# A two-layer trunk on one core: the low part of every third weight chunk made by ScalarE and an accumulating DMA

## The chip, the cores and the metric

One Trainium2 chip, one of its cores. The metric is the device time of one execution in microseconds (us), lower is better. The kernel before takes 1078.44 us (median of 2 runs, 1078.35 to 1078.53).

## What is computed

A trunk of two layers on 256 tokens of 1024 numbers in float32. Each layer is a SwiGLU, a mixer (differential attention in layer 0, retention in layer 1) and a second SwiGLU, each behind an RMS norm and added to the residual:

```python
h = x + 0.5 * _swiglu(_rms(x, ffn1_norm[i]), ffn1_w_in[i], ffn1_w_out[i])
xn = _rms(h, mix_norm[i])
m = _diff_attention(xn, ...) if kind == 0 else _retention(xn, ...)
h = h + m
x = h + 0.5 * _swiglu(_rms(h, ffn2_norm[i]), ffn2_w_in[i], ffn2_w_out[i])

def _swiglu(xn, w_in, w_out):            # w_in 1024 x 5632, w_out 2816 x 1024
    a, b = jnp.split(xn @ w_in, 2, axis=-1)
    return (jax.nn.silu(a) * b) @ w_out
```

Nearly all of the work is `x @ w` with a weight that is read once.

## The kernel before

**Products.** A float32 product is made of three products in float32r, a rounded format that TensorE takes at a higher rate. Both factors are split exactly: `hi` is the rounded value, `lo` is what is left of it. The sum is x_hi w_hi + x_lo w_hi + x_hi w_lo (`mm_tokens`, `mm_cols`; every matmul is issued at L263). In the SwiGLU's first product (`mm_cols`) the weights are stationary, and x_hi and x_lo stand side by side as 512 moving columns, so a block of 128 x 128 weights takes one matmul of 512 columns with `hi` and one of 256 with `lo`.

**Weights.** `Weights` (L96 to L173) cuts all weights into 180 chunks of 1 MB, 128 partitions by 2048 numbers, in the order of their use: chunk 0 and 1 are split in four pieces, the others in two pieces of 128 x 1024. Chunks 0 to 32 belong to the first SwiGLU (names f0: 22 chunks of `w_in`, which come in pairs, then 11 of `w_out`), 33 to 48 to the attention, 49 to 81 and 82 to 114 to the SwiGLUs f1 and f2, 115 to 146 to the retention, 147 to 179 to f3. There are three sets of buffers, four of each: `raw` (what the DMA loads from HBM), `hi` and `lo`. Chunk i goes through these steps:
- `load` (L120): SyncE's queue issues one DMA of 1 MB into `raw`; it needs the raw buffer of chunk i-4, that is, both pieces of that chunk have been split. `keep_order` holds SyncE to the order of issue, so a load that waits holds up those behind it.
- `round` (L136): ScalarE casts a piece of `raw` into `hi` (L150). The buffer was that of chunk i-4, so TensorE has to be done with that one.
- `remain` (L153): VectorE subtracts, lo = raw - hi (L157). After the last piece the raw buffer is given back and the next load is issued.
- `take`: TensorE's stream uses the chunk.

When each step is issued is decided while the program is written: `Flow` keeps an estimate of the time of TensorE's stream, and `paced` splits a further piece every 800 ns of it as far as there are buffers; `take` forces what is still missing. A scheduler then sets the order on each engine; an engine takes its instructions in that order, and one that waits holds up those behind it.

**SwiGLU.** For a pair of chunks (gate columns `wa`, value columns `wb`, 256 columns each) TensorE makes four passes of 16 matmuls: `pa`, `pb`, `pa`, `pb`, each into a bank of PSUM of its own (8 banks). Behind each pass ScalarE copies half of the bank (`rest`, L316) and VectorE adds the halves (L317); ScalarE applies SiLU (L469), VectorE multiplies (L477), and the result is split into `hT` (L311 on ScalarE, L312 on VectorE). Then `out_proj` multiplies with `w_out`, adds to the residual `h` (L411), and squares it (L333) for the next norm.

**Norm.** In `norm_transpose` VectorE adds the sums of squares (`v`, L351), GpSimd takes the power -0.5 (`r`, L343), VectorE scales (`xs`, L357), TensorE transposes (`pt`, L293), and the result is split into `xn`, which every product of the next part needs. A token tile's norm is done behind the last product of that tile. The norms of the attention's heads and of the retention use the same line L343. GpSimd does nothing else in the kernel before but set constants.

**Opening.** From 0 to about 36 us the order is written out by hand: chunks 0 and 1 in four pieces, the two norms, then chunks 2 and 3, whose products (`pa`, `pb`) follow the first `ps_f` products of chunks 0 and 1.

Of the kernel before, what the change touches and what calls it, by code (L numbers as in the profile page):

```python
# [15 lines left out]
ALU = mybir.AluOpType  # L16
# [4 lines left out]
T = 256  # L21
# [10 lines left out]
ROOT_D = 32.0  # L32
TAIL = 2

# Offsets in the table of constants: distances, decays.
C_DIST = 0
C_DEC = 384
C_END = C_DEC + RT_H * 384


def constants():
    """Causal distances (masked ones far away) for the query tiles side by side, and the
    retention's decays by head, keys on the partitions: key tile 0 with all queries, then
    key tile 1 with query tile 1."""
    c = np.zeros((P, C_END), np.float32)
    p = np.arange(P)[:, None]
    k = np.arange(T)[None, :]
    for off, n, q0 in ((0, P, 0), (P, T, P)):
        d = (q0 + p) - k[:, :n]
        c[:, C_DIST + off : C_DIST + off + n] = np.where(d >= 0, d, FAR)  # L50
    for h in range(RT_H):
        log_g = math.log(1.0 - 2.0 ** (-5.0 - h))
        d = k - p
        dec = np.where(d >= 0, np.exp(np.maximum(d, 0) * log_g), 0.0) / 16.0
        at = C_DEC + h * 384
        c[:, at : at + T] = dec
        c[:, at + T : at + 384] = dec[:, :P]
    return c


class Flow:
    """Order of issue: the main stream of products says how long each takes, and tasks (generators
    that yield the time their next step has to wait) are taken up in between when they are due."""

    def __init__(self):
        self.now, self.tasks, self.n = 0.0, [], 0
# [27 lines left out]


class Weights:  # L96
    """Chunks of the weights in the order of their use: loaded ahead, and split exactly into two
    float32r parts ahead, piece by piece, as far as there are buffers."""

    RAW, PARTS, PACE = 4, 4, 800  # L100

# [26 lines left out]
            self.raws.append(raw)  # L128

    def split(self):  # L130
        """Split a further piece if a buffer for it is there."""
        if self.round():
            self.remain()
            self.next = self.flow.now + self.PACE

    def round(self):  # L136
        if not self.todo:
            i = len(self.parts)
            if i >= min(len(self.specs), self.freed + self.PARTS):
                return False  # L140
            self.load()
            _, shape, pieces = self.specs[i]
            hi = self.pool.tile([P] + shape, F32R, tag="hi", name=f"hi{i}", bufs=self.PARTS)
            lo = self.pool.tile([P] + shape, F32R, tag="lo", name=f"lo{i}", bufs=self.PARTS)
            n = shape[0] // pieces
            self.todo = [(i, slice(k, k + n)) for k in range(0, shape[0], n)]
            self.parts.append((hi, lo))
        i, ks = self.todo.pop(0)
        self.rounded.append((i, ks, not self.todo))
        self.nc.scalar.copy(self.parts[i][0][:, ks, :], self.raws[i][:, ks, :])  # L150
        return True

    def remain(self):  # L153
        i, ks, last = self.rounded.pop(0)
        hi, lo = self.parts[i]
        raw = self.raws[i]
        self.nc.vector.tensor_tensor(lo[:, ks, :], raw[:, ks, :], hi[:, ks, :], ALU.subtract)  # L157
        if last:
            self.raws[i] = None
            self.load()  # L160
# [17 lines left out]


def keep_order(tc, start, *engines):  # L180
    """These engines (or all) take what has been issued since start in that order."""
    before = {}
    dep = mybir.DependencyInfo(mybir.DependencyClass.NoSync, mybir.DependencyReason.DATA)
    for ins in issued(tc)[start:]:
        if engines and ins.engine not in engines:
            continue
        if ins.engine in before:
            tc.add_manual_dep(ins, before[ins.engine], dep, reason="order")
        before[ins.engine] = ins.name
# [3 lines left out]
def trunk_kernel(ctx: ExitStack, tc: tile.TileContext, io, out: bass.AP):  # L193
# [15 lines left out]
    def blk(name, dtype, shape):  # L209
        return blkp.tile([P] + shape, dtype, tag="blk", name=name)  # L210

# [1 line left out]
    h = [act.tile([P, D], F32, tag=f"h{t}", name=f"h{t}") for t in range(NT)]  # L213

    def load_x(t):
# [11 lines left out]
    ones = const.tile([1, P], F32, name="ones")  # L227
    nc.vector.memset(ones, 1.0)

# [1 line left out]
    def plan_ffn(w_in, w_out):  # L231
        for j in range(FF // 256):
            pieces = 2 if wts.specs else 4
# [10 lines left out]
    w = io["da_w_in"][0]  # L244
# [6 lines left out]
    w = io["rt_w_in"][0]  # L251
# [6 lines left out]
        wts.rows(io["rt_w_out"][0], 2 * c)  # L258
    plan_ffn(io["ffn2_w_in"][1], io["ffn2_w_out"][1])

# [1 line left out]
    def mm(ps, lhsT, rhs, start, stop):  # L262
        nc.tensor.matmul(ps, lhsT=lhsT, rhs=rhs, start=start, stop=stop)  # L263
        flow.tick(7 + rhs.free_size() / 2.4 if lhsT.dtype == F32R else 7 + rhs.free_size() / 0.6)
# [1 line left out]
    xn = [None]  # L266

    def mm_tokens(ps, t, part, k0, nk, first, last):
        """ps[tokens, cols] += x[tokens, k0..] @ w, weights moving."""
        hi, lo = part  # L270
        for k in range(nk):
            xh = xn[0][:, k0 + k, t * P : (t + 1) * P]
            xl = xn[0][:, k0 + k, T + t * P : T + (t + 1) * P]
            mm(ps, xh, hi[:, k, :], first and k == 0, False)
            mm(ps, xl, hi[:, k, :], False, False)
            mm(ps, xh, lo[:, k, :], False, last and k == nk - 1)

    def mm_cols(ps, part, c):
        """ps[cols, 0:T] + ps[cols, T:2T] = (x @ w).T for 128 columns, weights stationary."""
        hi, lo = part  # L280
        cs = slice(c * P, (c + 1) * P)
        for k in range(KD):
            both = [
                (ps, hi[:, k, cs], xn[0][:, k, :], k == 0, k == KD - 1),
                (ps[:, :T], lo[:, k, cs], xn[0][:, k, :T], False, False),
            ]
            for args in reversed(both) if k == KD - 1 else both:
                mm(*args)
# [6 lines left out]
        return pt  # L295

    def proj_tokens(each, before=(None, None)):
        """x @ 512 columns by token tile; each(t, ps) takes the bank over."""
        ws = [wts.take() for _ in range(2)]
        for t in range(NT):  # L300
            if before[t] is not None:
                flow.join(before[t])
            ps = bank(f"pj{flow.n}_{t}")
            for i, part in enumerate(ws):
                mm_tokens(ps, t, part, 4 * i, 4, i == 0, i == 1)
                if t == NT - 1:
                    wts.free()
            each(t, ps)
# [7 lines left out]
        nc.scalar.copy(rest, ps[:, T:])  # L316
        nc.vector.tensor_tensor(out_ap, ps[:, :T], rest, ALU.add)  # L317

# [1 line left out]
    def load_gain(src, scale=1.0, n=D, tag="gain"):  # L320
        g = work.tile([P, n], F32, tag=tag, name=f"g{flow.n}_{src.tensor.name}", bufs=1)
        nc.sync.dma_start(g, src.partition_broadcast(P))
# [47 lines left out]
            flow.urgent -= 1  # L370

    def out_proj(nk, src, coef, name, gain, last=False):
        """h += coef * src @ w; begins the norm of h for the next part."""
        nch = nk // 2
        pieces = [[(0, 512), (512, 512)] for _ in range(NT)]
        if last:
# [15 lines left out]
        for c in range(nch - TAIL):  # L392
            part = wts.take()
# [5 lines left out]
        tasks = []  # L399
# [20 lines left out]
                tasks.append(flow.spawn(norm_transpose(t, xn[0], halves, name)))  # L420
        return tasks

# [1 line left out]
    def ffn(name, before, next_gain, last=False):  # L424
        hT = []

# [58 lines left out]
            last,  # L485
        )

# [1 line left out]
    def attention(before, next_gain):  # L489
        dist = const.tile([P, 384], F32, name="dist")  # L490
        nc.sync.dma_start(dist, io["consts"][:, C_DIST : C_DIST + 384])
# [19 lines left out]
        nc.vector.tensor_scalar(nlam, le[:, 1:2], le[:, 0:1], LAM_INIT, ALU.subtract, ALU.subtract)  # L511

        def grouped_norm(ps, ng, dim, name, w0, w1):
            """ps / rms over groups of dim columns, short of sqrt(dim)."""
            sq = work.tile([P, 512], F32, tag="xs", name=f"sq_{name}")
            nc.scalar.activation(sq, ps, AF.Square)
            ss = small.tile([P, ng], F32, tag=f"ss{ng}", name=f"ss_{name}")
            nc.vector.tensor_reduce(ss, sq.rearrange("p (g d) -> p g d", d=dim), AX.X, ALU.add)
            nc.vector.tensor_scalar_add(ss, ss, dim * EPS)
            r = inv_rms(ss, ng, name)  # L520
            yield w0
            qn = work.tile([P, 512], F32, tag="xs", name=f"qn_{name}")
            nc.vector.tensor_tensor(
                qn.rearrange("p (g d) -> p g d", d=dim),
                ps.rearrange("p (g d) -> p g d", d=dim),
                r.unsqueeze(2).broadcast_to([P, ng, dim]),
                ALU.mult,
            )
            yield w1
            return transposes(f"ptn_{name}", qn, 4).rearrange("p (j c) -> p j c", c=P)  # L530
# [16 lines left out]
        sides = (slice(0, P), slice(P, 384))  # L547

        def head(g, hh, qT, kT, need, wait, res):
            """One head's probabilities, transposed."""  # L550
            yield wait
            flow.join(*need)
            slope = 2.0 ** (-8.0 * (g * 4 + hh + 1) / DA_H)
# [2 lines left out]
            for m in range(2):  # L556
                name = f"{g}{hh}{m}"
                ms = slice(m * DH, (m + 1) * DH)
                ps = bank(f"s_{name}")
# [25 lines left out]
            a = work.tile([P, 384], F32, tag="att", name=f"att_{g}{hh}")  # L585
# [13 lines left out]
        aTs, oT = {}, {}  # L599

        def values(g, v, need, outs):
            """The heads' outputs, normed, transposed and split."""
            po = [bank(f"po_{g}{t}") for t in range(NT)]
            for hh in range(4):
                flow.join(need[hh])
# [28 lines left out]
        heads = {}  # L634
# [18 lines left out]

        return out_proj(KD, src, 1.0, "dao", next_gain)

# [1 line left out]
    def retention(before, next_gain):  # L657
        mT, done = [], []

        def mix(hd, v, qk, sg, sub, dec, pair):  # L660
            """One head's outputs, normed, gated, transposed and split."""
            yield 4000
            sT = bank(f"sT_{hd}")
            for cs, ks, qs in (
# [3 lines left out]
                for dk in range(2):  # L668
# [4 lines left out]
                        start=dk == 0,  # L673
# [53 lines left out]
        for hd in range(RT_H):  # L727
# [9 lines left out]
            for i in range(2):  # L737
                part = wts.take()
# [95 lines left out]
```

## Time and profile before

| | us |
|---|---|
| median of the runs | 1078.44 |
| the profiled execution: span from its first to its last instruction | 1076.2 |
| TensorE matmuls busy | 1065.4 (99%) |
| VectorE busy | 687.2 (64%) |
| ScalarE busy | 570.1 (53%) |
| GpSimd busy | 38.2 (4%) |
| share of the DMA engines' time that the loads take | 54.9% |

The span is what the profile covers; the median of the runs is 2.2 us above it (1078.44 - 1076.2), which is what lies around the span. "Busy" of TensorE holds modelled ends of pipelined matmuls. Engine names in rows: PE is TensorE (PEld its weight loads), DVE VectorE, ACT ScalarE, POOL GpSimd, SP or SPq SyncE and its queue. Names of tiles stand without their numbers in the profile: `lo<-raw,hi` is the subtraction of any chunk.

### The profile page before, as it was taken

What the parts mean: (1) busy time and instruction counts of PE and PEld (TensorE: products, weight loads), DVE (VectorE), ACT (ScalarE), POOL (GpSimd) and SP (SyncE); (2) the same over time, 40 slices, a digit from 0 to 9 for tenths busy, and PEclk for the clock granted to TensorE, in tenths of its full rate; (3) what the DMA queues carried; (4) which work ended last, traced back from release to release, by engine and by line L of the source; (5) the groups of instructions that cost most, each with busy time, mean ns of one, the idle gap of its engine ahead of it and who ended that gap; (6) DMA issues with size and microseconds to landing.
All of it is one profiled execution on the core that took longest, in us unless ns stands there. A gap on an engine that the chain in (4) does not pass through costs nothing.

```text
span 1076.2 us, 14437 instructions
## 1 busy us (share of the span) xinstructions
PE 1065.4 (99%) x5688; PEld 906.7 (84%) x5688; DVE 687.2 (64%) x1008; ACT 570.1 (53%) x949; POOL 38.2 (4%) x38
## 2 busy tenths in 40 slices
PE   8999999999999999999999999999999999999998
PEld 7888888877778888888888888888888888888887
DVE  6767654778876766646676654656655557676641
ACT  7556543556655656434565643455544445565530
POOL 0000000132010000000000000000000000000000
PEclk9999999999999999999999999999999999999999
DMA  9855655464337465554756465476456445646531
GB/s 310 260 193 161 217 198 190 141 221 139 123 105 241 159 209 180 198 193 138 234 170 213 166 206 195 139 240 209 152 176 219 157 157 180 212 157 199 195 115 40
DMA packets 133942, 196.57 MB, mean 183 GB/s; under 512 B 3825, under 2 KB 103153, under 8 KB 133874
## 3 DMA queue, kind: packets, MB, share of 16 engines
q1 hardware_dynamic: 133874, 195.64, 54.9%
q8 instruction: 45, 0.74, 0.3%
q14 instruction: 23, 0.19, 0.1%
HBM read 194.58 MB, written 1.05 MB: 182 GB/s over the span
## 4 chain that ended last, share of the span: by engine, by line
PE 94%; DVE 3%; POOL 1%; issue 1%; DMA 1%; ACT 0%; SPq 0%; POOLq 0%
PE pa_f L263 21%; PE pb_f L263 21%; PE pj L263 13%; PE y_f3o L263 6%; PE y_f1o L263 6%; PE y_f0o L263 6%; PE y_f2o L263 6%; PE pqk L263 4%; PE y_rto L263 4%; PE ps_f L263 3%; PE y_dao L263 2%; DVE lo L157 1%; PE rpo L690 1%; DMA raw<-in_ffn_w_in_dram 1%; PE po L615 0%
## 5 line engine op out<-in xcount | busy, mean ns | idle before, releaser
L157 DVE TENSOR_TENSOR lo<-raw,hi 128x1024 fp32r<-128x1024 f32 (+1 forms) x364 | 434.1, 1210 | 163.6 <-ACT hi L150 162.0
L150 ACT CAST hi<-raw 128x1024 fp32r<-128x1024 f32 (+1 forms) x364 | 366.2, 1040 | 162.4 <-PE y_f1o L263 25.8
L263 PE MATMUL pj<-hi,xn_f2o 128*128 128x512 f32 x256 | 81.1, 393 | 0.0
L317 DVE TENSOR_TENSOR b_f<-pb_f,rest_bf 128x256 f32<-128x256 f32 x80 | 33.7, 421 | 54.2 <-ACT rest_bf L316 54.2
L316 ACT COPY rest_af<-pa_f 128x256 f32<-128x256 f32 x80 | 29.9, 373 | 66.1 <-PE pa_f L263 66.1
L263 PE MATMUL pj<-hi,xn_f0o 128*128 128x512 f32 x192 | 62.6, 400 | 0.0
L317 DVE TENSOR_TENSOR a_f<-pa_f,rest_af 128x256 f32<-128x256 f32 x80 | 33.7, 421 | 42.6 <-ACT rest_af L316 42.6
L469 ACT ACTIVATE s_f<-a_f 128x256 f32<-128x256 f32 x80 | 33.3, 416 | 49.8 <-DVE a_f L317 49.8
L263 PE MATMUL pa_f<-xn_dao,hi 128*128 128x512 f32 x160 | 58.3, 398 | 0.0
L263 PE MATMUL pa_f<-xn_in,hi 128*128 128x512 f32 x160 | 58.3, 398 | 0.0
L263 PE MATMUL pa_f<-xn_f1o,hi 128*128 128x512 f32 x160 | 58.3, 398 | 0.0
L263 PE MATMUL pa_f<-xn_rto,hi 128*128 128x512 f32 x160 | 58.3, 398 | 0.0
L263 PE MATMUL pb_f<-xn_dao,hi 128*128 128x512 f32 x160 | 58.2, 398 | 0.0
L263 PE MATMUL pb_f<-xn_f1o,hi 128*128 128x512 f32 x160 | 58.2, 398 | 0.0
L263 PE MATMUL pb_f<-xn_rto,hi 128*128 128x512 f32 x160 | 58.2, 398 | 0.0
L263 PE MATMUL pb_f<-xn_in,hi 128*128 128x512 f32 x160 | 58.2, 398 | 0.0
L263 PE MATMUL y_f3o<-hi,hT_f 128*128 128x512 f32 (+1 forms) x220 | 56.7, 347 | 0.0
L263 PEld LDWEIGHTS pj<-hi,xn_f2o 128*128 128x128 f32 x256 | 48.1, 188 | 9.7
L263 PE MATMUL y_f1o<-hi,hT_f 128*128 128x512 f32 x176 | 54.6, 390 | 0.0
L263 PE MATMUL y_f0o<-hi,hT_f 128*128 128x512 f32 x176 | 54.6, 390 | 0.0
L263 PE MATMUL y_f2o<-hi,hT_f 128*128 128x512 f32 x176 | 54.6, 390 | 0.0
L311 ACT CAST hT_f<-g_f 128x256 fp32r<-128x256 f32 x80 | 32.6, 408 | 37.6 <-DVE g_f L477 37.6
(229 smaller groups left out, 2290.7 us busy)
## 6 DMA issues: line engine op xcount, KB each, us to landing
raw<-in_ffn_w_in_dram SPq DMA_DIRECT2D x86, 1024.0 KB, 5.2
raw<-in_ffn_w_out_dram SPq DMA_DIRECT2D x44, 1024.0 KB, 5.0
raw<-in_rt_w_in_dram SPq DMA_DIRECT2D x24, 1024.0 KB, 5.2
raw<-in_da_w_in_dram SPq DMA_DIRECT2D x12, 1024.0 KB, 5.3
raw<-in_rt_w_out_dram SPq DMA_DIRECT2D x8, 1024.0 KB, 4.9
raw<-in_da_w_out_dram SPq DMA_DIRECT2D x4, 1024.0 KB, 5.0
raw<-in_ffn_w_in_dram SPq DMA_DIRECT2D x8, 256.0 KB, 5.7
g_in_ffn_norm_dram<-in_ffn_norm_dram SPq DMA_DIRECT2D x3, 512.0 KB, 4.3
```

The source lines that it names most:

```text
L150: self.nc.scalar.copy(self.parts[i][0][:, ks, :], self.raws[i][:, ks, :])
L157: self.nc.vector.tensor_tensor(lo[:, ks, :], raw[:, ks, :], hi[:, ks, :], ALU.subtract)
L263: nc.tensor.matmul(ps, lhsT=lhsT, rhs=rhs, start=start, stop=stop)
L311: nc.scalar.copy(hi, src)
L316: nc.scalar.copy(rest, ps[:, T:])
L317: nc.vector.tensor_tensor(out_ap, ps[:, :T], rest, ALU.add)
L469: nc.scalar.activation(s, a, AF.Silu)
L690: nc.tensor.matmul(po[t], lhsT=lhs[:, cs], rhs=v[rhs][:, vt, :], start=first and lhs is ph and rhs == 0, stop=last and lhs is pl,)
```

## The change

For every chunk whose number leaves 2 when divided by 3 (2, 5, 8, ... 179; 60 of 180), ScalarE writes -1 times the raw piece into `lo`, rounded to float32r as `hi` is, so that `lo` holds -hi; then GpSimd issues a DMA that adds the raw words to it in place: lo = raw - hi. VectorE's subtraction of these chunks is gone. Nothing else differs but comments and docstrings, which are removed; lines behind them stand up to 6 higher.

```diff
     def round(self):
...
         i, ks = self.todo.pop(0)
         self.rounded.append((i, ks, not self.todo))
-        self.nc.scalar.copy(self.parts[i][0][:, ks, :], self.raws[i][:, ks, :])
+        hi, lo = self.parts[i]
+        self.nc.scalar.copy(hi[:, ks, :], self.raws[i][:, ks, :])
+        if i % 3 == 2:
+            self.nc.scalar.mul(lo[:, ks, :], self.raws[i][:, ks, :], -1.0)
         return True

     def remain(self):
         i, ks, last = self.rounded.pop(0)
         hi, lo = self.parts[i]
         raw = self.raws[i]
-        self.nc.vector.tensor_tensor(lo[:, ks, :], raw[:, ks, :], hi[:, ks, :], ALU.subtract)
+        if i % 3 == 2:
+            self.nc.gpsimd.dma_start(lo[:, ks, :], raw[:, ks, :], accum_op=ALU.add)
+        else:
+            self.nc.vector.tensor_tensor(lo[:, ks, :], raw[:, ks, :], hi[:, ks, :], ALU.subtract)
         if last:
             self.raws[i] = None
             self.load()
```

The rows below are the built programs' order on an engine; a tile's name carries its chunk (hi2 is chunk 2's high part) and a number of its own.

ScalarE in the opening, behind the casts of the second norm, before the change:

```order
L150 CAST hi2_232<-raw2_103 128x1024 x2
L150 CAST hi3_256<-raw3_105 128x1024 x2
L430 ACT_TABLE_LOAD
L430 ACTIVATE st_f00_275<-ps0_f00_186 128x256
L150 CAST hi4_295<-raw4_156 128x1024 x2
```

and now:

```order
L151 CAST hi2_232<-raw2_103 128x1024
L153 ACTIVATE lo2_233<-raw2_103 128x1024
L151 CAST hi2_232<-raw2_103 128x1024
L153 ACTIVATE lo2_233<-raw2_103 128x1024
L151 CAST hi3_258<-raw3_105 128x1024 x2
L436 ACT_TABLE_LOAD
L436 ACTIVATE st_f00_277<-ps0_f00_186 128x256
L151 CAST hi4_297<-raw4_156 128x1024 x2
```

Chunk 2's negated roundings stand between its casts, and chunk 3's casts move behind both.

ScalarE in the middle of f0, where chunks 16 and 17 (a pair) are split, before:

```order
L150 CAST hi16_987<-raw16_773 128x1024
L469 ACTIVATE s_f06_1_983<-a_f06_1_979 128x256
L150 CAST hi16_987<-raw16_773 128x1024
L316 COPY rest_bf06_1_1011<-pb_f06_1_985 128x256
L150 CAST hi17_1021<-raw17_807 128x1024 x2
L316 COPY rest_af07_0_1045<-pa_f07_0_1019 128x256
L311 CAST hT_f06_905<-g_f06_1_1014 128x256
```

and now:

```order
L151 CAST hi16_997<-raw16_781 128x1024
L475 ACTIVATE s_f06_1_993<-a_f06_1_989 128x256
L151 CAST hi16_997<-raw16_781 128x1024
L153 ACTIVATE lo17_1032<-raw17_815 128x1024
L322 COPY rest_bf06_1_1021<-pb_f06_1_995 128x256
L151 CAST hi17_1031<-raw17_815 128x1024 x2
L317 CAST hT_f06_915<-g_f06_1_1024 128x256
L153 ACTIVATE lo17_1032<-raw17_815 128x1024
L322 COPY rest_af07_0_1057<-pa_f07_0_1029 128x256
```

Chunk 17's first negated rounding stands ahead of the copy of `rest_b`, its second behind the cast of `hT`, which now stands ahead of `rest_a`.

GpSimd around the norm that follows f0 (`r_f0o0` and `r_f0o1` for the two token tiles, `r_q` for the attention's heads), before:

```order
L343 TENSOR_TENSOR r_in1_172<-v_in1_170,half_87 128x1
L343 TENSOR_TENSOR r_f0o0_1804<-v_f0o0_1802,half_87 128x1
L343 TENSOR_TENSOR r_f0o1_1857<-v_f0o1_1855,half_87 128x1
L343 TENSOR_TENSOR r_q00_1944<-ss_q00_1941,half_87 128x8
L343 TENSOR_TENSOR r_q01_1990<-ss_q01_1987,half_87 128x8
```

and now:

```order
L161 DMA lo29_1622<-raw29_1501 128x1024 x2
L161 DMA lo32_1720<-raw32_1599 128x1024 x2
L349 TENSOR_TENSOR r_f0o0_1826<-v_f0o0_1824,half_87 128x1
L161 DMA lo35_1942<-raw35_1697 128x1024
L349 TENSOR_TENSOR r_f0o1_1879<-v_f0o1_1877,half_87 128x1
L161 DMA lo35_1942<-raw35_1697 128x1024
L349 TENSOR_TENSOR r_q00_1968<-ss_q00_1965,half_87 128x8
```

The 120 DMAs of the change stand on GpSimd between the powers of the norms; 17 of the 32 powers now have one directly ahead.

## Rows read from the trace of the kernel before

**Rows 1.** The page's parts 1 and 2: engines' busy time; TensorE's granted clock by slice

```profile
PE 1065.4 (99%) x5688; PEld 906.7 (84%) x5688; DVE 687.2 (64%) x1008; ACT 570.1 (53%) x949; POOL 38.2 (4%) x38
...
PEclk9999999999999999999999999999999999999999
```

**Rows 2.** The chain of work that ended last, whole span, shares by line

```profile
by line: PE pa_f L263 21.0%; PE pb_f L263 20.9%; PE pj L263 12.6%; PE y_f3o L263 5.7%; PE y_f0o L263 5.6%; PE y_f1o L263 5.6%; PE y_f2o L263 5.6%; PE pqk L263 4.2%; PE y_rto L263 3.9%; PE ps_f L263 3.3%; PE y_dao L263 1.7%; DVE lo L157 0.8%
```

**Rows 3.** The same chain in f0, 92 to 110 us: start, us, engine's passes

```profile
104.45 2.82 PE pa_f L263 x16
107.27 2.82 PE pb_f L263 x16
```

**Rows 4.** VectorE's timeline there: start, us, instruction, [idle before it <- what ended it]

```profile
96.10 1.22 DVE L157 TENSOR_TENSOR lo<-raw,hi 128x1024 fp32r<-128x1024 f32 x1
```

**Rows 5.** ScalarE's timeline there (chunk 16's second cast, then chunk 17's two)

```profile
91.98 1.04 ACT L150 CAST hi<-raw 128x1024 fp32r<-128x1024 f32 x1
93.26 0.37 ACT L316 COPY rest_bf<-pb_f 128x256 f32<-128x256 f32 x1 [0.24 <-PE pb_f L263]
93.53 2.00 ACT L150 CAST hi<-raw 128x1024 fp32r<-128x1024 f32 x2
96.08 0.37 ACT L316 COPY rest_af<-pa_f 128x256 f32<-128x256 f32 x1 [0.55 <-PE pa_f L263]
```

**Rows 6.** Groups by line and shape: count, busy us, mean ns, idle before

```profile
L157 DVE TENSOR_TENSOR lo<-raw,hi 128x1024 fp32r<-128x1024 f32 x356 | 429.0, 1222 | 163.6 <-ACT hi L150 162.0
L150 ACT CAST hi<-raw 128x1024 fp32r<-128x1024 f32 x356 | 361.6, 1050 | 160.4 <-PE y_f1o L263 25.8 <-PE y_f0o L263 25.8 <-PE y_f2o L263 25.8
```

**Rows 7.** The page's part 3 (loads' queue), then stretches; last columns clock, DMA share, GB/s

```profile
q1 hardware_dynamic: 133874, 195.64, 54.9%
...
10.00:20.00 10.00, 9.64 (x63) 9.35 (x64) 8.86 (x14) 7.28 (x15) 0.56 (x1) 1.00 1.09 354
20.00:30.00 10.00, 10.00 (x73) 9.39 (x73) 9.30 (x12) 8.12 (x11) 0.00 (x0) 1.00 1.09 356
...
36.00:126.00 90.00, 90.00 (x512) 78.27 (x511) 62.51 (x97) 53.63 (x97) 0.00 (x0) 1.00 0.59 194
```

**Rows 8.** DMA issues: count, KB each, median us from issue to landing

```profile
raw<-in_ffn_w_in_dram SPq DMA_DIRECT2D x86, 1024.0 KB, 5.2
...
h<-in_x_dram SPq DMA_DIRECT2D x4, 256.0 KB, 2.8
```

**Rows 9.** Tile raw: duration ns min/median/max of an issue; casts' idle time, by releaser

```profile
L127 SPq DMA_DIRECT2D raw<-in_ffn_w_in_dram x94: 367/368/1524, 2.0 to 971.0; - x94
...
  DMA raw<-in_ffn_w_in_dram: 2.5, 4
```

**Rows 10.** ScalarE's timeline in the opening

```profile
17.85 3.90 ACT L150 CAST hi<-raw 128x1024 fp32r<-128x1024 f32 x4
21.77 1.28 ACT L430 ACT_TABLE_LOAD   x1
...
25.89 1.05 ACT L150 CAST hi<-raw 128x1024 fp32r<-128x1024 f32 x1 [0.56 <-DMA raw<-in_ffn_w_in_dram]
```

**Rows 11.** The chain of work that ended last, 0 to 30 us

```profile
17.33 7.80 PE ps_f L263 x65
25.13 0.71 PE pa_f L263 x4
```

**Rows 12.** The same chain at the norm behind f0, 186 to 330 us

```profile
199.86 1.22 DVE lo L157
201.32 1.48 POOL r_f0o L343
202.82 0.76 DVE xs_f0o L357
203.72 0.63 PE pt_f0o L293 x4
```

## The prediction

> **What bounds the kernel now.** I read the page's busy times and clock first. TensorE is busy 1065.4 of 1076.2 us, at a granted clock of full speed (the 2.4 GHz level) in every slice, while VectorE stands at 64% and ScalarE at 53% [rows 1]. Then the chain of waits: all the large entries are matmuls, and VectorE's subtraction, the thing the change takes away in part, holds 0.8% of it, 8.6 us [rows 2]. So the most that any change beside TensorE's stream can win is the 10.8 us in which TensorE is idle, 1.0%. A measurement of this kernel tells about 2% from no change, so a visible gain is as good as excluded, and the question is only whether the new path delivers `lo` in time.
>
> How much time it has is read in the middle of f0. The last subtraction of chunk 17 ends at 97.32 us (96.10 + 1.22) [rows 4]; the pass that first uses it starts at 107.27 [rows 3]. That is a lead of 10.0 us, and the pattern repeats every two chunks. The lead comes from the buffers: a chunk's cast begins as TensorE leaves the chunk four places earlier (the copies beside the casts wait for that same pass [rows 5]), and then four passes of 2.82 us, 11.3 us, stand between.
>
> The loads have slack too. Of 364 casts only 4 waited for a load, 2.5 us in all [rows 9].
>
> **The change part by part.** It touches 60 chunks, 120 pieces of 128 x 1024 float32 (0.524 MB).
>
> *VectorE* loses 120 x 1.222 us [rows 6] = 147 us and comes down to 541 us (50%). On the chain that is at best a third of 8.6 us, 2.9; but where a chunk of the change stands in a chain, as chunk 35 does at the norm behind f0 (199.86, then GpSimd's power at 201.32 [rows 12]), ScalarE's rounding and GpSimd's issue take the place of the subtraction. I take -1 us, between -3 and 0.
>
> *ScalarE* gains 120 x 1.05 us = 126 us, pricing the negated rounding as a cast of the same shape [rows 6]: 696 us, 65%. Its work behind a pass comes up to about 2 us later in the pair concerned. Hidden by the eight PSUM banks: a bank is filled in 2.82 us, so TensorE does not miss one for several passes. 0 us; in the attention, whose short chains run through ScalarE, I add 0.5 us.
>
> *The DMA itself.* The trace shows no DMA issued by GpSimd and none that adds, so I bound it. The loads take 54.9% of 1076.2 us for 195.64 MB [rows 7], 3.02 us of all engines per MB, so 0.524 MB costs 1.58 us each time it crosses them. From below: one crossing, 1.6 us, as a copy. From above: three, 4.7 us (read raw, read lo, write lo, one behind the other). I take two, 3.2 us, since two operands have to be read where a copy reads one. What is fixed around it follows from two loads: 1.049 MB lands in 5.2 us and 0.262 MB in 2.8 [rows 8], a slope of 3.05 us per MB, which leaves 2.0 us. The issue by GpSimd I take as 1 us, between SyncE's shortest, 0.37, and longest, 1.52 [rows 9]. A piece alone then lands 6.2 us after its rounding, between 4.0 and 8.2.
>
> The Trainium skill (Collectives: The Full Stack, "The bandwidth ceiling: the fold count and why AG ≠ RS ≠ AR") says that an add inside the DMA costs its second source read, half a copy's rate, and not the adder. By that the piece costs the two crossings I take, and the rival of three falls away; no run here shows such a DMA yet.
>
> In the steady part: chunk 17's first rounding can start when chunk 16's casts end at 93.0 (91.98 + 1.04 [rows 5]), and its second stands behind the copy of `rest_b`, two casts and the cast of `hT`, so it ends near 98.5. TensorE wants the second piece half a pass after the first, at 107.27 + 1.4 = 108.7. 10.2 us are there. Needed: 6.2 alone, or 9.3 if a whole load (1.049 MB, 3.2 us of the engines) goes ahead of it. No stall: 0 us for 58 chunks, with 1 to 4 us to spare. If this cover is gone, each missing microsecond counts up to 60 times. The raw buffer comes back some 6 us later than before; SyncE's queue holds the next loads behind that one, but casts hardly wait for loads now, and a buffer's circle has time: roundings 4 us, the addition 6 to 9, a load 5.2, together 15 to 18 of the 22.6 us that four chunks last (eight passes of 2.82).
>
> The engines' total: 120 x 3.2 = 380 us more on 591, 90% of the span. That fits, though not by much.
>
> *The opening* is the one place without lead. Chunk 2's casts start at 17.85 [rows 10]; its roundings end at about 19.9 and 21.9, and chunk 3's casts shift to 23.9; with a last subtraction its split ends at 25.2, and it is used a pass later, at 28.0. TensorE wants chunk 2's `lo` from 25.2 and its second piece from 26.6 [rows 11]. The DMA engines are full there: shares of 1.09 in both stretches, at 355 GB/s [rows 7], and chunk 5's load lands only at 25.89, as ScalarE waits for it [rows 10]. From 19.9 on they owe 6.0 us of loads and 6.4 us of additions; interleaved, they are done at about 32, so the second piece is some 5 us late, or 3.5 if it gets the larger share. I take +4.5 us; from below 0 (one crossing, ahead of the loads: 23.1 and then the fixed part), from above 10 (three crossings behind the loads). Afterwards chunk 6's load starts about 10 us later; it has 10 us of lead in `lo`, and TensorE itself is later, so nothing follows.
>
> The Trainium skill (DMA: Bandwidth & Descriptors, "Issuing engines are not separate DMA queues") says that DMAs issued by GpSimd run on the same 16 engines as SyncE's and interleave with them; it speaks against the change here. By it the opening costs the 4.5 us; with engines of their own the two pieces would land near 28 and cost about 1.5. Whether the trace agrees, only the changed kernel can show.
>
> Sum: -1 + 0.5 + 0 + 4.5 = +4 us. The profiled span 1076.2 becomes 1080.2, and with the 2.2 us around it 1082.4: 1082 us against 1078.44.
>
> **The rivals.**
>
> *The DMA engines become the bound (slower).* If a piece costs three crossings, the additions take 120 x 4.7 = 569 us on top of 591: 1160 us, more than the span. Then `lo` and the loads come late in every pair, and the time goes to about 1160. Place: all SwiGLU and retention stages; it decides from about 4 us per piece, where 591 + 120 x 4 = 1071 fills the span; shortly before that the 10.2 us of lead are used up. For it: no row shows the addition's price, and the engines already take 59% in the steady part of f0 [rows 7]. Against it: two crossings are the natural price.
>
> *GpSimd's queue holds up the norms.* 17 of the 32 powers stand directly behind a DMA that itself waits for a rounding. If each comes 1.5 us late on the chain, that is 25 us: 1104. For it: the power is on the chain [rows 12]. Against it: its DMA is issued when ScalarE's rounding ends, and that is mostly earlier than the norm's input; only five parts change over.
>
> *No cost at all.* The opening's addition gets ahead of the loads and VectorE's 2.9 us are won: 1075.5. Against it: the full engines at 10 to 30 us.
>
> **How the numbers follow.** My forecast (1077 to 1092) 0.63; the engines as the bound 0.24, anywhere from 1095 to 1160 and beyond; GpSimd's queue 0.08, at or under 1104; no cost 0.05. 2% lies at 1057 and 1100. Faster by over 2%: 0.01, since 10.8 us is all there is to win. Slower by over 2%: nearly all of 0.24 and half of 0.08, 0.27. Within: 0.72. The range runs from 1075 (the third rival) to 1140, which leaves out about a third of the first rival's weight and little else; the likeliest case alone is 1077 to 1092.
>
> **What would show it.** Right: TensorE's idle time up by 3 to 6 us, all of it before 40 us, with `pa_f` waiting for a DMA; the passes in the middle of f0 still 2.82 us apart without gaps; VectorE near 541 and ScalarE near 696 us busy; a new queue with some 63 MB and a share near 35%. Wrong: `pa_f`, `pb_f` or `y` waiting for a DMA of `lo` in pair after pair, casts waiting for loads, a DMA share at 95% or above; or powers on GpSimd waiting behind DMAs with TensorE idle at the norms. Wrong on the other side: a time under 1075, which would need TensorE's passes themselves to be shorter.

## The result and the profile after

The changed kernel takes 1085.08 us (median of 2 runs, 1084.38 to 1085.78) against 1078.44: 1.0062 times the time before, with a 95% interval of 1.0045 to 1.008. By the bound of 2% that is no change; the interval says that it is 6.6 us, and slower.

The page's parts 1 to 3 of the changed kernel (busy time; TensorE's granted clock by slice; DMA queues with packets, MB and their share of 16 engines):

```profile
PE 1068.2 (99%) x5688; PEld 908.1 (84%) x5688; DVE 553.9 (51%) x888; ACT 675.4 (62%) x1069; POOL 138.9 (13%) x158
...
PEclk9899999999999999999999999999999999999999
...
q1 hardware_dynamic: 133874, 195.64, 54.4%
q0 software_dynamic: 17280, 62.92, 29.6%
```

Beside [rows 1, 7]: VectorE is down from 687.2 to 553.9 us, ScalarE up from 570.1 to 675.4, and a second queue has 62.92 MB (120 pieces of 0.524). TensorE still does the same 5688 matmuls. The span is 1082.6 us, so a piece takes 0.296 x 1082.6 / 120 = 2.67 us of all engines. One slice of the clock, the second, is not full, and that is the place to look at. The first of TensorE's waits for others, whole span (us in total, times, longest us), and the only one for an addition:

```profile
PE pa_f L269 <- DMA lo<-raw: 4.1, 2, 3.9
```

For 120 additions TensorE waits twice, both times in `pa_f`. The chain from 16 to 40 us shows where:

```profile
21.78 10.72 DMA lo<-raw
...
32.55 2.31 PE pa_f L269 x7
34.86 2.78 PE pb_f L269 x16
```

This is chunk 2. Its second piece is issued at 21.78 and lands 10.72 us later; TensorE wanted it at 26.6. TensorE's timeline there, and GpSimd's two issues:

```profile
29.01 0.58 PE L269 MATMUL pa_f<-xn_in,lo 128*128 128x256 f32 x1 [3.92 <-DMA lo<-raw]
29.39 0.63 PE L269 MATMUL pa_f<-xn_in,hi 128*128 128x512 f32 x1
...
32.55 0.58 PE L269 MATMUL pa_f<-xn_in,lo 128*128 128x256 f32 x1 [0.19 <-DMA lo<-raw]
...
34.70 0.39 PE L269 MATMUL pb_f<-xn_in,hi 128*128 128x512 f32 x1
```

```profile
19.90 1.03 POOL L161 DMA_DIRECT2D lo<-raw  x1 [5.81 <-ACT lo L153]
21.78 0.88 POOL L161 DMA_DIRECT2D lo<-raw  x1 [0.85 <-ACT lo L153]
```

The bracket is what to read: 3.92 us idle before the first `lo`, 0.19 before the second piece. In between a matmul of 512 columns takes 0.63 us where it takes 0.39 from 34.70 on. The stretches say why (busy by engine PE, PEld, DVE, ACT, POOL, then granted clock, DMA share, GB/s):

```profile
20.00:30.00 10.00, 6.08 (x45) 5.66 (x44) 5.15 (x5) 8.50 (x10) 1.80 (x2) 0.88 1.09 300
26.00:34.00 8.00, 4.80 (x15) 3.82 (x15) 3.12 (x4) 5.49 (x7) 1.34 (x2) 0.61 1.08 284
...
36.00:126.00 90.00, 90.00 (x513) 78.31 (x512) 50.17 (x84) 61.75 (x106) 8.69 (x10) 1.00 0.92 258
```

TensorE stood idle for 3.9 us, and in that gap the granted clock fell to the lower level (1.2 GHz); the mean over 26 to 34 us is 0.61. Before the change the same eight microseconds had no gap:

```profile
26.00:34.00 8.00, 8.00 (x48) 7.00 (x47) 5.75 (x10) 4.27 (x9) 0.00 (x0) 1.00 1.10 349
```

From 36 to 126 us it is busy without a gap again, with the DMA engines at 0.92 where they had 0.59 [rows 7]. The pass of [rows 3] at 107.27 now stands at 113.97, one of a chain without gaps:

```profile
111.15 2.82 PE pa_f L269 x16
113.97 2.82 PE pb_f L269 x16
116.79 2.82 PE pa_f L269 x16
```

So 6.7 us are lost by 34.70 us (that first pass of `pb_f` would have begun at 26.6 + 1.4 = 28.0), the same 6.7 stand in the middle of f0, and the span is longer by 1082.6 - 1076.2 = 6.4. By this profile the whole cost is in the opening. Of the 6.4, TensorE's idle time holds 3.6 (14.4 us against 10.8), and 2.8 are matmuls that took longer (1068.2 against 1065.4). Landings of all DMAs (KB each, median us from issue to landing), with [rows 8]:

```profile
raw<-in_ffn_w_in_dram SPq DMA_DIRECT2D x86, 1024.0 KB, 7.8
lo<-raw POOLq DMA_DIRECT2D x120, 512.0 KB, 7.6
```

A load lands 2.6 us later than before, but by ScalarE's waits only 3 casts waited for one, 1.6 us in all, where 4 did before [rows 9].

### The profile page after: what moved, and what is told of

Same layout as the page of the kernel before. It is cut to its first block, busy times and chain, and to the rows that moved or that the text cites. A ratio compares the mean times of both kernels' runs of the same rounds, so it can differ in the third digit from the quotient of the medians.

```text
span 1082.6 us, 14825 instructions
## 1 busy us (share of the span) xinstructions
PE 1068.2 (99%) x5688; PEld 908.1 (84%) x5688; DVE 553.9 (51%) x888; ACT 675.4 (62%) x1069; POOL 138.9 (13%) x158
## 3 DMA queue, kind: packets, MB, share of 16 engines
q1 hardware_dynamic: 133874, 195.64, 54.4%
q0 software_dynamic: 17280, 62.92, 29.6%
HBM read 194.58 MB, written 1.05 MB: 181 GB/s over the span
## 4 chain that ended last, share of the span: by engine, by line
PE 92%; issue 2%; ACT 2%; DMA 1%; DVE 1%; POOL 1%; SPq 0%; ACTq 0%; POOLq 0%; DVEq 0%
PE pb_f L269 21%; PE pa_f L269 21%; PE pj L269 13%; PE y_f3o L269 6%; PE y_f2o L269 6%; PE y_f0o L269 5%; PE y_f1o L269 5%; PE pqk L269 4%; PE y_rto L269 4%; PE ps_f L269 3%; PE y_dao L269 1%; DMA lo<-raw 1%; PE rpo L696 1%; DMA raw<-in_ffn_w_in_dram 1%; PE po L621 0%
## 5 line engine op out<-in xcount | busy, mean ns | idle before, releaser
L163 DVE TENSOR_TENSOR lo<-raw,hi 128x1024 fp32r<-128x1024 f32 (+1 forms) x244 | 288.7, 1204 | 185.3 <-ACT hi L151 183.7
L161 POOL DMA_DIRECT2D lo<-raw x120 | 104.6, 871 | 789.8 <-ACT lo L153 345.4
L153 ACT ACTIVATE lo<-raw 128x1024 fp32r<-128x1024 f32 x120 | 127.0, 1058 | 18.2 <-PE pa_f L269 9.3
```

The costliest lines, as they stand in the source:

```text
L153: self.nc.scalar.mul(lo[:, ks, :], self.raws[i][:, ks, :], -1.0)
L161: self.nc.gpsimd.dma_start(lo[:, ks, :], raw[:, ks, :], accum_op=ALU.add)
```

## The experiments

The theory after the result: chunk 2 alone costs the 6.6 us, because its additions share full DMA engines with the loads of the opening; the other 59 chunks cost nothing, since the engines as a whole are not full. The rivals: the loss is spread and only looks like the opening; the addition is slow by itself; the fall of the clock, not the wait, is what costs. The condition on `i` stands twice in the kernel, in `round` and in `remain`; a diff that changes it shows one of the two, and both are changed.

**Without chunk 2.** Time before on that chip, for this run, the next two and that of two of three chunks: 1077.99 us (1077.11 to 1078.89, 13 runs).

```diff
-        if i % 3 == 2:
+        if i % 3 == 2 and i > 2:
```

> The change without its first chunk: chunk 2 goes back to VectorE, the other 59 chunks stay on the new path. Theory A, all of the change's 6.6 us come from chunk 2 in the opening: the time goes back to 1078.4 us, within 1.5, TensorE waits nowhere for the added words and its granted clock is full throughout. Rival B, the cost is spread over the 60 chunks (ScalarE's extra 127 us, the fuller DMA engines, GpSimd's queue): the time stays at 1083 to 1085.

Measured: 1078.54 us (10 runs), 1.0002 [0.9993, 1.0012]. The same stretch, and the first of TensorE's waits, where no `lo` is left:

```profile
26.00:34.00 8.00, 8.00 (x48) 6.95 (x48) 3.23 (x9) 6.78 (x13) 1.90 (x2) 1.00 1.12 340
```

```profile
PE ptn_o L299 <- DVE qn_o L529: 1.5, 3, 0.9
```

59 of the 60 chunks cost nothing, within 0.13%. They win nothing either, though VectorE is at 52% in this run.

**Chunk 2 alone.**

```diff
-        if i % 3 == 2:
+        if i == 2:
```

> The new path for chunk 2 alone; the other 59 chunks are subtracted by VectorE as before. Theory A: 1084 to 1086 us, the whole cost from one chunk, with the wait of about 4 us and the clock at half for about 7 us again. Rival B: 1079 to 1080.

Measured: 1084.06 us (4 runs), 1.0058 [1.0043, 1.0073]. TensorE's largest wait, and the stretch:

```profile
PE pa_f L269 <- DMA lo<-raw: 3.7, 1, 3.7
```

```profile
26.00:34.00 8.00, 4.35 (x18) 3.80 (x19) 5.66 (x7) 4.32 (x6) 0.00 (x0) 0.79 0.95 247
```

One chunk of 180 carries the whole cost. The lower clock came back for a shorter time than expected, 0.79 on the mean where the whole change has 0.61, and the cost is nearly the same.

**A busy TensorE in the wait.** 36 transposes into a bank that nobody reads stand ahead of chunk 2's first product, so that TensorE is not idle while the first piece is on its way.

```diff
+            if name == "f0" and j == 1:
+                begin = len(issued(tc))
+                busy = bank("busy")
+                for _ in range(36):
+                    nc.tensor.transpose(busy[:, :P], ident, ident)
...
```

What is not shown keeps TensorE to that order.

> The change, with 36 more transposes of the identity (into a bank that nothing reads) on TensorE ahead of chunk 2's first product, some 3.9 us of work at 0.109 each, so that TensorE is not idle while it waits for the addition. Theory C, of the 6.6 us about 4 are the wait and 2.7 the half clock that follows the idle time: the granted clock stays full and the time is 1082.4 us. Rival D, the words themselves come 6.6 us late and the slow clock only fills time in which TensorE would wait anyway: the wait grows by 2 to 3 us at the second piece and the time stays at 1085.

Measured: 1084.85 us (4 runs), 1.0067 [1.005, 1.0084]. The stretch 26 to 34 us, and TensorE's timeline:

```profile
26.00:34.00 8.00, 7.59 (x58) 6.92 (x58) 3.82 (x6) 6.74 (x11) 1.74 (x2) 1.00 1.07 271
```

```profile
26.06 4.09 PE L470 MATMUL busy<-ident 128*128 128x128 f32 x36
29.91 0.47 PE L269 MATMUL pa_f<-xn_in,hi 128*128 128x512 f32 x1
...
32.42 0.39 PE L269 MATMUL pa_f<-xn_in,lo 128*128 128x256 f32 x1 [0.41 <-DMA lo<-raw]
...
33.70 0.39 PE L269 MATMUL pb_f<-xn_in,hi 128*128 128x512 f32 x1
```

The clock stays full, and nothing is won: the second piece lands at 32.4 as before, and a faster TensorE waits 0.41 us there in place of 0.19. The wait did not grow by the 2 to 3 us that were expected, since the transposes hold TensorE until 29.91, where it had gone on at 29.01. The slow clock filled time in which TensorE would have waited. What it can have cost is what lies behind that landing, 34.70 - 33.70 = 1.0 us in these two profiles; the timed runs do not show even that.

**Loads held back.** Chunk 2 alone again, but GpSimd copies one column of its second piece into the buffers of chunks 4 and 5 before their loads, which overwrite it (`gate` is that column; nothing is left out). So these two loads start when the piece has landed, and with them all that SyncE issues behind them. The time before was 1078.11 us (20 runs) on that chip, for this run and those of every second chunk, of every chunk, and of chunks 35, 51 and so on.

```diff
...
+            if i in (4, 5):
+                self.nc.gpsimd.tensor_copy(raw[:, 0, 0:1], self.gate)
             for k in range(0, shape[0], n):
                 self.nc.sync.dma_start(raw[:, k : k + n, :], src[:, k : k + n, :])
...
```

What is not shown sets `gate`, makes chunk 4 wait for it, and puts `i == 2` in the two conditions.

> Only chunk 2 takes the new path, and the loads of chunks 4 and 5 start after its second piece has landed (a copy of one column on GpSimd, overwritten by the load, holds them back). Theory J (in the opening the pieces were late because the loads shared the engines): the first piece lands 4.5 to 6 us after its issue, at about 25, the second at 26.5 to 28, in place of 29.0 and 32.5; TensorE waits for chunk 2 by at most 1 us, and the time is 1078.5 to 1081, unless chunks 4 and 5 now come late, which would show as waits of TensorE behind 34 us. Rival K (the first additions take 9 to 11 us whatever the engines do, by GpSimd's queue): the pieces still land at about 29 and 32.5, and the time is 1084 or more.

Measured: 1078.43 us (10 runs), 1.0003 [0.9994, 1.0013]. The landings of the two pieces (min, median, max), and the chain:

```profile
DMA to landing us min/median/max: 4.8/5.2/5.6
```

```profile
21.31 5.61 DMA lo<-raw
...
26.96 1.44 PE pa_f L277 x7
```

The addition takes 4.8 and 5.6 us instead of 9.1 (29.0 - 19.9) and 10.7, and the cost is gone. It was SyncE's transfers beside it. The addition's own speed and GpSimd's queue are out as causes. The run takes away more than the two loads, though: the next norm's weights (`g_in_mix_norm`, 0.524 MB), issued at 17.78 and landed 14.3 us later in the changed kernel, are issued at 10.43 here, ahead of the loads, so the share of each transfer is not told apart.

**Two of three chunks.** How far the engines can be filled.

```diff
-        if i % 3 == 2:
+        if i >= 6 and i % 3:
```

> The new path for two of three chunks from chunk 6 on (116 chunks, 232 pieces), none in the opening. The prediction's rival of the DMA engines as the bound, tried at a higher dose: at 2.65 us of all engines a piece (29.6% of 1082.6 us over 120), 615 us come on top of the loads' 590, 1205 us in all, more than the span: the time is 1205 us or above and TensorE waits for added words in the steady part. Rival E, the lead of 10 us covers it: 1078 to 1090. In between, 1100 to 1200, ScalarE's extra 244 us (to about 815, 75%) or the loads' lateness would have to be read from the waits.

Measured: 1215.7 us (4 runs), 1.1281 [1.1259, 1.1303]. Queues, and TensorE's largest wait:

```profile
q0 software_dynamic: 33408, 121.65, 51.7%
q1 hardware_dynamic: 133874, 195.64, 48.2%
```

```profile
PE pb_f L269 <- DMA lo<-raw: 47.7, 40, 2.5
```

The shares add up to 99.9%, and TensorE waits for `lo` 40 times in the 80 passes of `pb_f`: the DMA engines are the bound. A piece takes 0.517 x 1214.3 / 232 = 2.71 us, so loads and additions are 0.999 x 1214.3 = 1213 us, where the expectation had 1205; ScalarE is busy for 64%.

**Every second chunk.**

```diff
-        if i % 3 == 2:
+        if i >= 6 and i % 2 == 0:
```

> Every second chunk from chunk 6 on (87 chunks, 174 pieces) takes the new path, the opening none. At the 2.67 us of all engines per piece that the change's profile gives, the additions take about 462 us beside some 590 us of loads: 1052 us, 97 to 98% of the span. Theory E (the DMA engines cost nothing until their total passes the span): 1078 to 1085, ratio 1.000 to 1.006, TensorE waiting for lo and for casts by under 5 us in all. Rival F (landings grow by queueing well before the engines are full, and the 10 us of lead in lo are used up): 1095 to 1130, TensorE waiting for a DMA of lo in many pairs.

Measured: 1123.08 us (4 runs), 1.0417 [1.0392, 1.0441]. Queues, TensorE's two largest waits, and three stretches:

```profile
q1 hardware_dynamic: 133874, 195.64, 53.0%
q0 software_dynamic: 25056, 91.24, 42.7%
```

```profile
PE pb_f L269 <- DMA lo<-raw: 6.8, 8, 1.2
PE pa_f L269 <- DMA lo<-raw: 5.8, 7, 1.4
```

```profile
36.00:126.00 90.00, 87.32 (x495) 75.39 (x494) 40.15 (x73) 62.64 (x105) 13.35 (x16) 1.00 0.95 248
186.00:330.00 144.00, 133.57 (x653) 104.78 (x653) 79.91 (x179) 97.53 (x180) 38.26 (x34) 0.98 0.85 232
570.00:640.00 70.00, 67.93 (x381) 58.19 (x380) 32.65 (x60) 50.22 (x84) 10.31 (x12) 1.00 1.03 264
```

The change's own share is 54.4 + 29.6 = 84%, and free but for the opening; 95.7% costs 4.2%. That share is one of a span that has already grown: 0.957 x 1120.4 = 1072 us of transfers (2.75 us a piece), 99.6% of the 1076.2 before. The loss comes in small waits in many places, not at one. Theory E, by which only a total above the span costs, falls for the program as a whole, and rival F's time came. For a stage by itself it is not refuted: from 36 to 126 us every third chunk took the share from 0.59 to 0.92, so every second one would take it to about 1.08 (an estimate, 0.59 + 0.33 x 1.5), more than the stretch holds, while in other stretches the engines have room (0.85 from 186 to 330 us). Loads are late too: ScalarE waited for them 60 times, 153 us in all, where the kernel before has 4 waits and 2.5 us [rows 9]. Late pieces, late buffers and full stretches are not told apart by this run.

**Every chunk.** One run.

```diff
-        if i % 3 == 2:
+        if i >= 6:
```

> Every chunk from chunk 6 on (174 chunks, 348 pieces) takes the new path. Theory A (a piece takes 2.65 to 2.67 us of all engines whatever the load): 590 + 348 x 2.65 to 2.67 = 1512 to 1519 us of the engines, which are busy nearly throughout, so 1515 to 1540. Rival (the price falls when several additions are in flight, or rises when they meet): under 1480 or over 1570.

Measured: 1440.07 us, under the theory's range and in the rival's (under 1480).

```profile
q0 software_dynamic: 50112, 182.47, 64.2%
q1 hardware_dynamic: 133874, 195.64, 39.8%
```

The rival's reason is not it: a piece takes 0.642 x 1438.1 / 348 = 2.65 us, as the theory had it. But the shares add up to 104%, as the opening's reach 1.09 before the change, with loads alone [rows 7]. So the packets' times overlap, within one queue too, and 1.00 is not where the share ends; the sum of shares taken as a time (1.04 x 1438.1 = 1496 us) comes out too long by 4%.

**The norms.** VectorE's second subtraction of chunks 35, 51, 84, 117 and 149 stands beside GpSimd's power of a norm. Only these chunks, and as a control five others:

```diff
-        if i % 3 == 2:
+        if i in (35, 51, 84, 117, 149):
```

> Only chunks 35, 51, 84, 117 and 149 take the new path, those whose subtraction stands on VectorE in the chain of a norm that TensorE waits for. Theory G (the subtraction lengthens these chains, and taking it off VectorE is the gain that the change hides): 1075 to 1077, ratio 0.997 to 0.999. Rival H (ScalarE's second rounding and GpSimd's issue take its place, or the chain is not shortened): 1078 to 1080, ratio 1.000 to 1.002.

```diff
-        if i % 3 == 2:
+        if i in (25, 41, 74, 107, 139):
```

> Five chunks take the new path as in the run before last, but chunks 25, 41, 74, 107 and 139, whose subtraction is beside no norm that TensorE waits for. Theory G (what was gained with chunks 35, 51, 84, 117 and 149 came from the norms' chains): no gain here, 1077.5 to 1078.8, ratio 0.999 to 1.001. Rival H (five chunks off VectorE gain anywhere): 1076 to 1077, ratio 0.998 to 0.999.

Measured: 1076.48 us (11 runs), 0.9986 [0.9977, 0.9995], the best of all; the control 1078.22 us (11 runs), 1.0 [0.9991, 1.0009], on another chip, beside 1078.06 there (21 runs). So some 1.6 us (0.5 to 2.5) are to be had at the norms and none at these five other places. The chain at the norm behind the attention in the first of these two runs:

```profile
317.69 0.92 POOL lo L161
318.61 0.61 POOL r_dao L349
```

The power ends 0.61 us after the issue ahead of it. Before, the same norm has 1.48:

```profile
317.62 1.48 POOL r_dao L343
```

TensorE's busy time around this norm (314 to 330 us) goes from 15.44 us to 15.80.

**The second pieces alone**, on the thought that they are what holds up the power:

```diff
-        if i % 3 == 2:
+        if ks.start and i in (35, 51, 84, 117, 149):
```

> Only the second pieces of chunks 35, 51, 84, 117 and 149 take the new path; the first pieces stay on VectorE. Before, the second subtraction starts on VectorE just before GpSimd's power of the second token tile, and that power takes 1.40 to 1.47 us where the first tile's takes 0.55. Theory L (the power is held up by the subtraction beside it): with the second subtraction gone, the power takes 0.55 us at all five norms, 0.85 to 0.92 us less each, 4.4 us in all if nothing else comes late: 1073.5 to 1075, ratio 0.9955 to 0.997. Rival M (the power is slow for another reason, or its chain is then set by ScalarE's casts and negated rounding): 1076 to 1078.5, with powers of 1.4 us or gaps on TensorE as long as before.

Measured: 1078.4 us (11 runs, beside the same 1078.06), 1.0004 [0.9995, 1.0012]. The powers of the norm behind f1, before and now (min, median, max ns of its two):

```profile
L343 POOL TENSOR_TENSOR r_f1o<-v_f1o,half x2: 552/1006/1459, 498.1 to 504.9; 128x1 f32<-128x1 f32 x2
```

```profile
L349 POOL TENSOR_TENSOR r_f1o<-v_f1o,half x2: 549/556/562, 498.8 to 505.5; 128x1 f32<-128x1 f32 x2
```

The mechanism is as expected, 1.46 us down to 0.56, and the price is not: TensorE stood idle for only 0.55 us in front of these transposes, and the changed order puts something else late. VectorE in front of that norm, before and now:

```profile
499.37 0.74 DVE L357 SCALAR_TENSOR_TENSOR xs_f1o<-h,r_f1o,g_in_ffn_norm_dram 128x512 f32<-128x512 f32 x1
500.03 0.68 DVE L411 SCALAR_TENSOR_TENSOR h<-y_f1o,h 128x512 f32<-128x512 f32 x1
```

```profile
499.38 1.42 DVE L363 SCALAR_TENSOR_TENSOR xs_f1o<-h,r_f1o,g_in_ffn_norm_dram 128x512 f32<-128x512 f32 x2 [0.69 <-POOL r_f1o L349]
500.71 0.68 DVE L417 SCALAR_TENSOR_TENSOR h<-y_f1o,h 128x512 f32<-128x512 f32 x1
```

The scheduler now puts both halves of the first tile's scaling ahead of the addition to `h`, which is 0.68 us later, and the norm's chain behind it. TensorE's busy time rises around two norms as much as with the whole chunks (15.86 us from 314 to 330, and 14.87 from 500 to 515, where the kernel before has 14.46 and the whole chunks 14.84), but not at the one behind the retention (14.42 from 880 to 895, against 14.39 and 14.78). Why the second halves gain nothing in all where the whole chunks gain 1.6 us is not settled by this.

## Why the prediction was right

The forecast of 1082 (likeliest case 1077 to 1092) met 1085.08, and "within 2%" came true. By its steps:

- *What bounds the kernel.* Right: TensorE's stream. VectorE's load fell by 133 us (147 were forecast) and nothing was won.
- *VectorE, -1 us.* Not shown by itself. Without chunk 2 the change is at 1.0002 [0.9993, 1.0012], -0.8 to +1.3 us, where the first three terms together made -0.5.
- *ScalarE, +126 us.* Measured 675.4 - 570.1 = 105 us. The negated rounding takes 1.06 us, close to the 1.05 priced, and the group's own sum is 127.0; but back to back the instructions overlap (in the opening a cast of 1.05 us starts at 17.57 and the rounding behind it at 18.52). It had no part in the time.
- *The piece at 3.2 us of all engines.* Mis-sized: 2.67 us, 1.7 crossings of 1.58 where I took two; the bounds of 1.6 and 4.7 held. The landing was close: 6.2 us alone, with the issue, was forecast, and 4.8 and 5.6 from the issue were measured with the loads held back. The Trainium skill (Collectives: The Full Stack, "The bandwidth ceiling: the fold count and why AG ≠ RS ≠ AR") says of ReduceScatter that its add costs a second source read and so half a copy's rate. The trace of this other kind of add comes near: 2.67 us against 1.58 is 0.59 of a load's rate. The rival of three crossings is out.
- *The steady part, 0 us.* Right, and for the reason given: the pass at 107.27 comes at 113.97 in a chain without gaps, and no matmul but the two in the opening waits for a `lo`, though the median landing is 7.6 us.
- *The opening, +4.5 us.* The place, the wait and its cause were right, the size was 6.7. TensorE wanted the second piece at 26.6 and it landed at 32.51, 5.9 us late. The prediction's own sum gives nearly that, 19.9 + 6.0 + 6.4 = 32.3, or 5.7 us; it calls this "some 5" and then takes 4.5, toward the 3.5 "if it gets the larger share". That choice is the term that was too small: the piece did not get the larger share. That the sum itself came out is partly luck: two pieces took 5.3 us of the engines and not 6.4, and the next norm's weights, 0.524 MB that SyncE issued at 17.78, were left out (1.6 us, an estimate at the loads' 3.02 us per MB). The rest, 34.70 - 32.51 = 2.2 us for the half pass that was reckoned at 1.4, is the lower clock, which the prediction did not have. The Trainium skill (DMA: Bandwidth & Descriptors, "Issuing engines are not separate DMA queues") says that DMAs run on the same 16 engines and interleave, whichever engine issued them. The trace agrees: with the loads held back the pieces take 4.3 and 5.1 us less from issue to landing.
- *The DMA engines as the bound.* It did not happen at this dose, 84% where 90% was reckoned, and it does happen at higher ones: every second chunk costs 4.2%, two of three 12.8%. The prediction let it decide where the sum fills the span, at 1071 us. Every second chunk makes 1072 us, that very line, and costs 45 us; so the cost begins below it, somewhere above the 909 us (0.84 x 1082.6) that were free. Where, no run shows.
- *GpSimd's queue at the norms.* It did not come true: the norm's first product stands at 210.44 against 204.35, 6.1 us later, not more than the 6.7 before it.

```profile
207.40 0.89 POOL lo L161
208.29 0.60 POOL r_f0o L349
...
210.44 0.24 PE pj L269
```

The power does stand behind a DMA's issue, as the rival had it, but ends 0.60 us after it, where before the power took 1.48 [rows 12].

## What to carry to other kernels

Work taken off an engine that nobody waited for won nothing here; what it cost was decided where its replacement had no lead, one chunk of 60. Ask for each such place what else is on the way through the DMA engines: the same addition took 5 us with SyncE's transfers out of the way and 10 beside them, and holding the loads back for some microseconds cost nothing. Set the transfers against the span before the change: 909 us of 1076 were free with 10 us of lead, 1072 were not.

## What was not expected

- GpSimd's power of 128 numbers takes 0.55 us, but 1.40 to 1.47 us where VectorE's second subtraction starts just ahead of it, at all five norms; with that subtraction gone, 0.55 to 0.56 at all five. The Trainium skill (SBUF — State Buffer, "SBUF: two separate sides") says that a VectorE instruction with two inputs in SBUF and a GpSimd instruction that reads SBUF keep each other out of a port they share, for a whole instruction. The runs agree: the subtraction reads `raw` and `hi`, and the power is longer by 0.9 us beside it.
- In a gap of 3.9 us TensorE's granted clock fell to the lower level, and a matmul of 512 columns took 0.63 us in place of 0.39, until about 34.4 us. By two profiles it cost 1.0 us at most, since the data were late anyway.
- The shares of the DMA queues add up to 104% where every chunk from 6 on is split by DMA, so a share of 1.00 is not yet the ceiling.
